# Rows broadcast through DRAM instead of on GpSimd, with merge and router issued in written order

## The chip, the cores and the metric

The kernel runs on one core of a Trainium2 chip. The metric is the device time of one execution in microseconds (us), as the median of the timed runs. Engines are named as in the profile: PE (TensorE), DVE (VectorE), ACT (ScalarE), POOL (GpSimd) and SP (SyncE, whose queue issues every DMA of this kernel).

## What is computed

One encoder layer for 256 tokens of width 1024, in float32:

```
mod = silu(c) @ w_ada + b_ada          # six rows of 1024: shift, scale, gate, twice
h   = x * (1 + scale1) + shift1
z   = h @ w_in                         # q, k, v of branch A; low-rank q, kv of branch B; gates g_a, g_b
y_a, y_b = chunked attention, latent attention
merged = sigmoid(g_a) * (y_a @ w_branch_a) + sigmoid(g_b) * (y_b @ w_branch_b)
x = layer_norm(2**0.25 * x + gate1 * (merged @ w_out), ln1_g, ln1_b)
h = x * (1 + scale2) + shift2
f = mixture of experts: top 4 of 32 by h @ w_router + b_router, clamped SwiGLU experts
x = layer_norm(2**0.25 * x + gate2 * f, ln2_g, ln2_b)
```

The expert weights are by far the most data: 32 experts of three 1024x1024 matrices, 402.7 MB. All of them are read.

## The kernel before

SBUF holds twenty blocks of 128x2048 float32 (1024 KB each). Every weight goes through them: `al()` gives the block that was freed longest ago, `fr()` frees one, and `hold(4)` sets four aside for the first expert loads. A load can start only when the last reader of its block is done. SP issues the DMAs in one queue, so a load that waits for its block keeps the later ones back.

The work comes in stages. The attention stage computes z and both attentions; a weight is split there into a rounded part and a rest (`split`, L152 to L154: ACT casts, then DVE or POOL subtracts, as its argument says), and `mm3` (L278 to L281) makes three matmuls of it. `ada2` gathers the modulation rows on DVE, and `z_pair` makes the gate columns g0 to g7.

The **merge** follows, and it is where the change lies. `mod_rows` (L714) sums the modulation rows on PE, adds the bias on DVE, and writes the second shift and scale to a DRAM buffer `rowd`, from which four small loads bring them back as columns. `load_branch(jp)` loads and splits a quarter of both branch weights. The loop over jp (L773) makes tiles ba and bb on PE (48 matmuls of 256 columns, four banks of PSUM for two quarters), multiplies them by the gates on DVE (L788 to L790) and splits the result into mgh and mgl. `mod_gates` (L733) spreads the rows gate1 and gate2 over 128 partitions with four `partition_broadcast` on POOL, called at jp 1. `mod_cols` (L745) scales the router's weights, and `mod_sums` (L756) makes two row sums on PE.

Then **output projection and router**: `load_wo` loads and splits a quarter of w_out, `o_part(t, hf, i)` is 12 matmuls of 512 columns for token half t and column half hf, `resid` adds the residual, `r_T` transposes it and makes router logits, `stats`, `normalise` and `route` make the normalised x (`xn`), the choice of experts and the one-hot matrix `pt0`, `gather_first` gathers the tokens of the first two experts (tiles sxg), `weigh` and `first_norm` make the routing weights and the residual of the second norm.

The **experts** run in 14 groups: s, then e0 to e12. A group loads gate, up and down weights in 1024 KB blocks (L1012) and computes tiles sg, su, sd (L1056). Here the gathered tokens are first scaled into `xgb` (L1044 on ACT, L1046 on DVE). `load_norm` at the end spreads ln2_g and ln2_b with two more `partition_broadcast`.

What sets the order: the kernel is built with a scheduler that simulates time and moves instructions within each engine, SP's DMAs among them, as

```
with _tile.TileContext(nc, schedule_with_timeline_sim=True) as tc:
```

says, and `tc.issue_after` bounds it at two places.

Of the kernel before, what the change touches and what calls it, by code (L numbers as in the profile page):

```python
# [70 lines left out]
def tile_layer(  # L71
# [583 lines left out]

    def load_branch(jp):
# [21 lines left out]
    for i in range(4):  # L678
# [6 lines left out]
        if i == 3:  # L685
            ms_v, ms_r = al()
# [28 lines left out]
    def mod_rows():  # L715
# [46 lines left out]

    G.memset(ones_p, 1.0)
    mod_rows()
    hold(4)
    load_branch(1)
    for b in range(2):
        A.activation(gT[b], gT[b], AF.Sigmoid)
    mgh_v, mgh_r = al(F32R)
    mgl_v, mgl_r = al(F32R)  # L770
    mgh = mgh_v.rearrange("p (j n) -> p j n", j=8)
    mgl = mgl_v.rearrange("p (j n) -> p j n", j=8)
    for jp in range(4):  # L773
# [9 lines left out]
        if jp + 2 < 4:  # L783
            load_branch(jp + 2)
# [7 lines left out]
        if jp == 1:  # L792
            rwa_v, rwa_r = al()
            gate1, g1r = rwa_v[:, 0:D], rwa_v[:, D:2 * D]
            b1r = p3.tile([P, D], F32, name="b1r")
            SP.dma_start(g1r, bcast_rows(ln1_g[0]))
            SP.dma_start(b1r, bcast_rows(ln1_b[0]))
            mod_gates()
        if jp == 2:
            mod_cols()  # L800
        if jp == 3:
            mod_sums()
            for j in range(3):
                G.tensor_copy(sel0[32 * j:32 * j + 32, :, :], ident[0:E, E - 2:E].unsqueeze(2).to_broadcast([E, 2, CAP]))
# [3 lines left out]
    WO = []  # L808

    def load_wo(hf, i):  # L810
        v, r = al()
        v = v.rearrange("p (k m) -> p k m", k=4)
        SP.dma_start(v, w_out[0, i * 512:(i + 1) * 512, hf * 512:(hf + 1) * 512].rearrange("(k p) m -> p k m", p=P))
        hv, hr = al(F32R)
        lv, lr = al(F32R)
        hi = hv.rearrange("p (k m) -> p k m", k=4)
        lo = lv.rearrange("p (k m) -> p k m", k=4)
        for q in range(2):
            ks = slice(2 * q, 2 * q + 2)
# [39 lines left out]
    def r_T(t, hf):  # L859
        ps = ps_b(f"rT{t}_{hf}")  # L860
        for q in range(2):
# [3 lines left out]
            A.copy(rT[:, 4 * hf + 2 * q:4 * hf + 2 * q + 2, :].rearrange("p a n -> p (a n)"), ps[:, q * 256:(q + 1) * 256])  # L865
        if hf == 0:
            lgps.append(ps_b(f"lg{t}"))
        for k in range(4 * hf, 4 * hf + 4):
            last = T.matmul(lgps[t][:, 0:E], rT[:, k, :], wrs[:, k, 0, :], start=(k == 0), stop=(k == 7))
        return last  # L870

    def stats(t):
# [15 lines left out]
    def route(t):  # L888
# [11 lines left out]
        ps = ps_b(f"cum{t}")  # L900
        if t == 1:
            T.matmul(ps[:, 0:E], ones_bf, mask_bf[:, 0, :], start=True, stop=False)
        T.matmul(ps[:, 0:E], tri, mask_bf[:, t, :], start=(t == 0), stop=True)
        V.tensor_mul(posm[:, t, :], ps[:, 0:E], mask_bf[:, t, :])
        last = V.tensor_tensor(pt0[:, t, :].rearrange("p (a n) -> p a n", a=2),
                        iota_s[:, 0:CAP].unsqueeze(1).to_broadcast([P, 2, CAP]),
                        posm[:, t, E - 2:E].unsqueeze(2).to_broadcast([P, 2, CAP]), op=ALU.is_equal)
        m8s.append(m8)
        ohs.append(oh)
        return last  # L910
# [23 lines left out]

    def gather_first(t):
# [9 lines left out]
    G.memset(zero_bf, 0.0)  # L945
    for i in range(2):
# [3 lines left out]
        load_wo(1, i)  # L950
# [4 lines left out]
    r_T(0, 0)  # L955
    resid(0, 1)
    o_part(1, 1, 0)
    fr(*WO[2][2:4])
    stats(0)
    r_T(0, 1)  # L960
    r_T(1, 0)
    o_part(1, 1, 1)
    fr(*WO[3][2:4])
    normalise(0)
    route(0)
    resid(1, 1)
    r_T(1, 1)
    gather_first(0)
    stats(1)
    routed = route(1)  # L970
    normalise(1)
# [17 lines left out]
    xgb = [mp.tile([P, 8, P], F32, name=f"xgb{i}") for i in range(2)]  # L989
# [35 lines left out]
    def expert_group(nm, segs, slots, wcol, get_w, get_bias, hooks=(), end=None):  # L1025
# [6 lines left out]
        for i in range(2):  # L1032
            if slots is not None:
# [5 lines left out]
            else:  # L1039
                ps = gps[i]  # L1040
            for kk in range(4):
                k = 4 * i + kk
                if kk % 2 == 0:
                    A.activation(xg[:, k, :], ps[:, kk * P:(kk + 1) * P], AF.Identity, bias=bc[:, k:k + 1], scale=gc[:, k:k + 1])  # L1044
                else:
                    V.tensor_scalar(xg[:, k, :], ps[:, kk * P:(kk + 1) * P], gc[:, k:k + 1], bc[:, k:k + 1],  # L1046
                                    op0=ALU.mult, op1=ALU.add)
# [192 lines left out]
    def load_norm():  # L1240
        fin_v, o_v = al()[0], al()[0]
        lnr = o_v[0:1, :].rearrange("p (a n) -> p a n", a=2)
        SP.dma_start(lnr[:, 0, :], ln2_g)
        SP.dma_start(lnr[:, 1, :], ln2_b)
# [130 lines left out]
```

## Time and profile before

| | |
|---|---|
| median of 3 runs | 1246.0 us (1244.69 to 1246.91) |
| profiled execution: its time | 1242.76 us |
| profiled execution: its span, first to last instruction | 1241.1 us |
| PE busy, share of the span | 1096.4 us, 88% |
| DVE, ACT, POOL busy | 375.4, 180.5, 102.2 us |
| mean granted TensorE clock | 0.954 of full speed |
| DMA moved | 462.51 MB |

The span begins with the first instruction; all positions below are microseconds from there. The attention stage ends at about 198 us, merge, projection and router run to about 284 us, and the experts from there to the end. A row of the trace gives start, duration, engine, line, operation and tiles, how many instructions it merges, and in brackets how long the engine sat idle before and what ended that.

### The profile page before, as it was taken

To read this page: it belongs to the slowest core of one execution; us is meant where nothing else is said; L and a number is where in the kernel's file an instruction comes from. 1 tells how busy PE (TensorE), PEld (TensorE's weight loads), DVE (VectorE), ACT (ScalarE), POOL (GpSimd) and SP (SyncE) were. 2 spreads that over 40 slices of the span, in tenths; PEclk is the share of its full clock that TensorE was granted. 3 is DMA by queue.
4 is the path that set the end of the run, shared out by engine and by line. 5 is a ranking of instruction groups with operands and counts; after the bars stand their busy time and mean duration, and the time that the engine had idled before them with its cause. 6 is when DMAs were issued, how large, how long until landed. Compare 5 with 4: busy or idle time off the path is not lost.

```text
span 1241.1 us, 19489 instructions
## 1 busy us (share of the span) xinstructions
PE 1096.4 (88%) x7991; PEld 534.1 (43%) x7991; DVE 375.4 (30%) x752; ACT 180.5 (15%) x364; POOL 102.2 (8%) x126
## 2 busy tenths in 40 slices
PE   5889896788898999999989889888898989898995
PEld 4659886763243333534323232232233434343431
DVE  4768984564122121212111011020021212121213
ACT  3346454321000000000000000000000000000011
POOL 2211553310000000000000000000000000000000
PEclk8989998889999999799999999999999999998998
DMA  9969567398999999999999999999999999999991
GB/s 339 321 214 331 179 232 244 136 400 322 418 419 419 418 419 419 419 419 419 418 420 419 421 417 420 419 420 419 418 420 418 419 419 418 420 419 418 420 389 67
DMA packets 93281, 462.51 MB, mean 373 GB/s; under 512 B 11499, under 2 KB 36120, under 8 KB 42246
## 3 DMA queue, kind: packets, MB, share of 16 engines
q1 hardware_dynamic: 93190, 461.24, 92.4%
q8 instruction: 64, 1.05, 0.3%
q14 instruction: 27, 0.22, 0.0%
HBM read 460.15 MB, written 1.06 MB: 372 GB/s over the span
## 4 chain that ended last, share of the span: by engine, by line
DMA 43%; PE 42%; DVE 7%; issue 2%; SPq 2%; ACT 2%; POOL 1%; ACTq 0%; DVEq 0%; POOLq 0%
DMA blk<-in_w_up_dram 14%; DMA blk<-in_w_gate_dram 13%; DMA blk<-in_w_down_dram 13%; DVE blk L642 1%; PE e11d L1056 1%; PE e12u L1056 1%; PE e1d L1056 1%; PE sd L1056 1%; PE e12d L1056 1%; PE e3d L1056 1%; PE e3g L1056 1%; PE e2d L1056 1%; PE e0d L1056 1%; PE e12g L1056 1%; PE e0u L1056 1%
## 5 line engine op out<-in xcount | busy, mean ns | idle before, releaser
L154 POOL TENSOR_TENSOR blk<-blk,blk 128x512 fp32r<-128x512 f32 (+2 forms) x44 | 82.6, 1895 | 145.1 <-ACT blk L153 71.7
L1303 POOL COPY sel<-sel 96x64 bf16<-96x64 bf16 (+2 forms) x30 | 5.9, 229 | 837.4 <-PE e6d L1136 90.5
L153 ACT CAST blk<-blk 128x512 fp32r<-128x512 f32 (+2 forms) x76 | 54.0, 766 | 62.1 <-DVE blk L790 16.2
L154 DVE TENSOR_TENSOR blk<-blk,blk 128x512 fp32r<-128x512 f32 (+2 forms) x32 | 43.7, 1377 | 30.3 <-ACT blk L153 21.1
L1096 ACT ACTIVATE blk<-blk 128x512 f32<-128x512 f32 x28 | 17.2, 630 | 218.0 <-DVE blk L1094 217.9
L642 DVE SCALAR_TENSOR_TENSOR blk<-blk,csil,blk 128x1024 f32<-128x1024 f32 x28 | 41.3, 1509 | 0.0
L279 PE MATMUL g<-blk,blk 128*128 128x256 f32 x128 | 38.7, 302 | 2.3 <-ACT blk L153 2.3
L281 PE MATMUL g<-blk,blk 128*128 128x256 f32 x128 | 38.6, 304 | 1.8 <-POOL blk L154 1.4
L280 PE MATMUL g<-blk,blk 128*128 128x256 f32 x128 | 38.3, 300 | 0.0
L1056 PE MATMUL e6u<-blk,blk 128*32 128x512 f32 x128 | 25.4, 599 | 4.1 <-DMA blk<-in_w_up_dram 4.1
L1056 PE MATMUL e7u<-blk,xgb 128*32 128x512 f32 x128 | 25.4, 599 | 4.1 <-DMA blk<-in_w_up_dram 4.1
L1056 PE MATMUL e5u<-blk,xgb 128*32 128x512 f32 x128 | 25.3, 599 | 4.1 <-DMA blk<-in_w_up_dram 4.1
L281 PEld LDWEIGHTS g<-blk,blk 128*128 128x128 f32 x128 | 26.2, 206 | 3.6 <-POOL blk L154 1.6
L279 PEld LDWEIGHTS g<-blk,blk 128*128 128x128 f32 x128 | 26.5, 207 | 2.8 <-ACT blk L153 2.5
L280 PEld LDWEIGHTS g<-blk,blk 128*128 128x128 f32 x128 | 26.5, 207 | 0.8 <-issue 0.8
L1056 PE MATMUL e4d<-blk,blk 128*32 128x512 f32 x128 | 23.0, 642 | 2.9 <-DMA blk<-in_w_down_dram 2.9
L1056 PE MATMUL e5d<-blk,xgb 128*32 128x512 f32 x128 | 22.8, 598 | 3.1 <-DMA blk<-in_w_down_dram 2.8
L1056 PE MATMUL e7d<-blk,blk 128*32 128x512 f32 x128 | 22.7, 598 | 3.1 <-DMA blk<-in_w_down_dram 2.8
L1056 PE MATMUL e6d<-blk,xgb 128*32 128x512 f32 x128 | 22.8, 636 | 2.7 <-DMA blk<-in_w_down_dram 2.7
L281 PE MATMUL bb<-blk,blk 128*128 128x256 f32 x32 | 10.7, 334 | 14.1 <-POOL blk L154 14.1
L1056 PE MATMUL e6g<-blk,blk 128*32 128x512 f32 x128 | 20.8, 596 | 1.7 <-DMA blk<-in_w_gate_dram 1.7
L1056 PE MATMUL e7g<-blk,xgb 128*32 128x512 f32 x128 | 19.8, 596 | 1.7 <-DMA blk<-in_w_gate_dram 1.7
(741 smaller groups left out, 1937.3 us busy)
## 6 DMA issues: line engine op xcount, KB each, us to landing
blk<-in_w_gate_dram SPq DMA_DIRECT2D x128, 1024.0 KB
blk<-in_w_up_dram SPq DMA_DIRECT2D x128, 1024.0 KB
blk<-in_w_down_dram SPq DMA_DIRECT2D x126, 1024.0 KB
blk<-in_w_ada_dram SPq DMA_DIRECT2D x24, 1024.0 KB
blk<-in_w_in_dram SPq DMA_DIRECT2D x12, 1024.0 KB
blk<-in_w_in_dram SPq DMA_DIRECT2D x8, 592.0 KB
blk<-in_w_out_dram SPq DMA_DIRECT2D x4, 1024.0 KB
blk<-in_w_branch_a_dram SPq DMA_DIRECT2D x4, 512.0 KB
```

The source lines that it names most:

```text
L153: A.copy(hi, src)
L154: (V if eng == "V" else G).tensor_sub(lo, src, hi.bitcast(F32))
L279: T.matmul(o, sh, mh, start=first, stop=False)
L280: T.matmul(o, sh, ml, start=False, stop=False)
L281: T.matmul(o, sl, mh, start=False, stop=last)
L642: eng.scalar_tensor_tensor(acc_v[:, sl], v[:, q * D:(q + 1) * D], csil[:, k:k + 1], acc_v[:, sl], op0=ALU.mult, op1=ALU.add)
L1056: T.matmul(pss[hf][c0:c0 + m, :], stat[:, k, c0:c0 + m], ch[par][k // 2][:, k % 2, hf * 512:(hf + 1) * 512], start=(k == 0), stop=(fine an ...
L1096: A.activation(s, g[:, sl], AF.Sigmoid, scale=SW_ALPHA)
L1303: G.tensor_copy(sel[:, lo:lo + n], sel96[:, r:r + 1].to_broadcast([96, n]))
```

## The change

POOL's broadcasts go. `rowd` gets four rows; gate1 and gate2 are loaded from it, and ln2_g and ln2_b from their inputs, by DMAs that read one row for all 128 partitions (`bcast_rows`). From `mod_rows` to `first_norm` the order of PE, ACT, DVE and POOL is the order in which the code is written (`tc.manual_schedule`); SP's order is still the scheduler's. Loading and splitting of branch and output weights are separate functions, and the raw loads are called earlier. `mod_cols` moves behind the merge loop. Logits, counting and placing are functions of their own, and the first tokens' scaling (`evacuate`) is called ahead of `weigh` and `first_norm`, in the written part.

```diff
     def load_branch(jp):
...
+        WB_raw.append((v, r))
+
+    def split_branch(jp):
+        v, r = WB_raw[jp]
         hv, hr = al(F32R)
...
         if i == 3:
-            load_branch(0)
+            split_branch(0)
+            load_branch(1)
...
-        rowd = dram.tile([2, D], F32, name="rowd")
-        for i in range(2):
+        rowd = dram.tile([4, D], F32, name="rowd")
+        for n, (st, j) in enumerate(((0, 2), (1, 0), (0, 0), (1, 2))):
             for hf in range(2):
-                j = 2 * (1 - i) + hf
-                SP.dma_start(rowd[i:i + 1, hf * 512:(hf + 1) * 512], rows32[32 * j:32 * j + 1, i, :])
+                SP.dma_start(rowd[n:n + 1, hf * 512:(hf + 1) * 512], rows32[32 * (j + hf):32 * (j + hf) + 1, st, :])
...
-    def mod_gates():
-        for i, dst in enumerate((gate1, gate2)):
-            for hf in range(2):
-                j = 2 * i + hf
-                G.partition_broadcast(dst[:, hf * 512:(hf + 1) * 512], rows32[32 * j:32 * j + 1, i, :])
+        SP.dma_start(gate1, bcast_rows(rowd[2]))
+        SP.dma_start(gate2, bcast_rows(rowd[3]))
...
+    engines = {e.engine for e in (T, A, V, G)}
+    order_cm = tc.manual_schedule(engines=engines)
+    order_cm.__enter__()
     G.memset(ones_p, 1.0)
...
     mod_rows()
-    hold(4)
-    load_branch(1)
+    split_branch(1)
     for b in range(2):
         A.activation(gT[b], gT[b], AF.Sigmoid)
+    load_branch(2)
+    split_branch(2)
+    hold(4)
...
-        if jp + 2 < 4:
-            load_branch(jp + 2)
+        if jp == 0:
+            load_branch(3)
+            split_branch(3)
+        else:
+            load_wo((jp - 1) // 2, (jp - 1) % 2)
...
-            mod_gates()
-        if jp == 2:
-            mod_cols()
-        if jp == 3:
-            mod_sums()
...
+        if jp in (1, 2):
+            split_wo()
+    mod_cols()
+    mod_sums()
...
     gather_first(1)
+    xg0 = keep.tile([P, 8, P], F32, name="xgb0")
+    evacuate(xg0, gps)
     for t in range(2):
-        with tc.issue_after(routed.ins):
-            weigh(t)
+        weigh(t)
     for t in range(2):
-        with tc.issue_after(routed.ins):
-            first_norm(t)
+        first_norm(t)
+    order_cm.__exit__(None, None, None)
...
-        G.partition_broadcast(g2r, lnr[:, 0, :])
-        G.partition_broadcast(b2r, lnr[:, 1, :])
+        SP.dma_start(g2r, bcast_rows(ln2_g[0]))
+        SP.dma_start(b2r, bcast_rows(ln2_b[0]))
```

Three places show what the new order is. The first is DVE at the start of the merge, before (tiles mod are the modulation rows, ba and bb the first quarter's products, L154 a split's subtraction):

```order
L721 TENSOR_TENSOR blk_180_1825<-mod_0_1987,blk_180_1825 128x512
L154 TENSOR_TENSOR blk_216_2075<-blk_214_2071,blk_215_2074 128x1024
L721 TENSOR_TENSOR blk_180_1825<-mod_1_1993,blk_180_1825 128x512
L788 TENSOR_TENSOR blk_133_1257<-blk_133_1257,ba_2021 128x512
L154 TENSOR_TENSOR blk_208_2012<-blk_206_2008,blk_207_2011 128x1024
L789 TENSOR_TENSOR blk_165_1608<-blk_165_1608,bb_2022 128x512
L790 TENSOR_TENSOR blk_133_1257<-blk_133_1257,blk_165_1608 128x512
L747 TENSOR_SCALAR c_98<-c_98 128x16
```

and DVE at the same place in the changed kernel (blk_194, blk_211 and blk_219 are the raw weights of quarters 1, 2 and 3):

```order
L729 TENSOR_TENSOR blk_181_1828<-mod_0_1994,blk_181_1828 128x512
L729 TENSOR_TENSOR blk_181_1828<-mod_1_2000,blk_181_1828 128x512
L154 TENSOR_TENSOR blk_209_2022<-blk_194_1908,blk_208_2021 128x1024
L154 TENSOR_TENSOR blk_213_2033<-blk_211_2029,blk_212_2032 128x1024
L154 TENSOR_TENSOR blk_221_2096<-blk_219_2092,blk_220_2095 128x1024
L824 TENSOR_TENSOR blk_133_1257<-blk_133_1257,ba_2042 128x512
L825 TENSOR_TENSOR blk_165_1608<-blk_165_1608,bb_2043 128x512
L826 TENSOR_TENSOR blk_133_1257<-blk_133_1257,blk_165_1608 128x512
```

The splits of quarters 1, 2 and 3 now all stand ahead of the first multiplication by a gate, and the column work (L747) is gone from here.

The second is SP's queue in the same stretch, before (c is the tile of columns, blk_220 quarter 3's raw weights, blk_224 the rows gate1 and ln1_g):

```order
L727 DMA rowd<-blk_180_1825 1x512 x2
L660 DMA blk_220_2135<-in_w_branch_a_dram 128x4x256
L727 DMA rowd<-blk_180_1825 1x512 x2
L660 DMA blk_220_2135<-in_w_branch_b_dram 128x4x256
L730 DMA c_98<-rowd 128x8
L731 DMA c_98<-rowd 128x8x1
L730 DMA c_98<-rowd 128x8
L731 DMA c_98<-rowd 128x8x1
L796 DMA blk_224_2149<-in_ln_g_dram 128x1024
L813 DMA blk_234_2282<-in_w_out_dram 128x4x512
```

and SP's queue in the changed kernel (blk_219 is quarter 3, blk_225 and blk_231 the first two quarters of w_out):

```order
L734 DMA rowd<-blk_181_1828 1x512 x8
L737 DMA c_98<-rowd 128x8
L738 DMA c_98<-rowd 128x8x1
L737 DMA c_98<-rowd 128x8
L738 DMA c_98<-rowd 128x8x1
L739 DMA blk_205_1992<-rowd 128x1024
L740 DMA gate_1983<-rowd 128x1024
L662 DMA blk_219_2092<-in_w_branch_a_dram 128x4x256
L662 DMA blk_219_2092<-in_w_branch_b_dram 128x4x256
L791 DMA blk_225_2156<-in_w_out_dram 128x4x512
L791 DMA blk_231_2219<-in_w_out_dram 128x4x512
```

Quarter 3 stood between the row writes and ahead of the column loads; it now stands behind eight row writes, four column loads and the two broadcasts.

The third is DVE at the end of the router, before (w, nm are `weigh`'s tiles, x_sb is written by `first_norm`; the scaling L1046 of the first tokens comes 23 instructions further on):

```order
L905 TENSOR_TENSOR pt_2302<-iota_s,posm 128x128
L916 TENSOR_SCALAR w_0_2574<-m_0_2495 128x4
L916 TENSOR_SCALAR w_1_2586<-m_1_2550 128x4
L929 SCALAR_TENSOR_TENSOR x_sb<-xn,blk_224_2149 128x1024 x2
L919 RECIPROCAL w_0_2574<-w_0_2574 128x4
L919 RECIPROCAL w_1_2586<-w_1_2586 128x4
L931 SCALAR_TENSOR_TENSOR x_sb<-b1r,x_sb 128x1024 x2
```

and in the changed kernel:

```order
L928 TENSOR_TENSOR pt_2305<-iota_s,posm 128x128
L962 TENSOR_SCALAR xgb_2578<-sxg_2527,c_98 128x128 x2
L962 TENSOR_SCALAR xgb_2578<-sxg_2529,c_98 128x128 x2
L936 TENSOR_SCALAR w_0_2587<-m_0_2494 128x4
L939 RECIPROCAL w_0_2587<-w_0_2587 128x4
L940 TENSOR_TENSOR w_0_2587<-w_0_2587 128x4
```

The scaling of the first tokens follows directly on the one-hot matrix pt, and `weigh` and `first_norm` come behind it.

## Rows read from the trace of the kernel before

**Rows 1.** Page: GB/s moved, in 40 slices of 31.0 us.
```profile
GB/s 339 321 214 331 179 232 244 136 400 322 418 419 419 418 419 419 419 419 419 418 420 419 421 417 420 419 420 419 418 420 418 419 419 418 420 419 418 420 389 67
```
**Rows 2.** Windows: stretch, its us, engines' busy us, clock, DMA share, GB/s.
```profile
240.00:280.00 40.00, 34.12 (x177) 28.95 (x175) 26.57 (x76) 10.04 (x18) 7.36 (x3) 0.88 0.95 368
280.00:300.00 20.00, 17.05 (x138) 7.12 (x141) 10.70 (x30) 2.10 (x7) 0.00 (x0) 0.90 0.70 275
```
**Rows 3.** Timeline of SP's queue: issues of loads, merge to first experts.
```profile
199.71 0.55 SPq L727 DMA_DIRECT2D rowd<-blk  x2
...
204.27 0.46 SPq L730 DMA_DIRECT2D c<-rowd  x1
...
206.85 1.18 SPq L796 DMA_DIRECT2D blk<-in_ln_g_dram  x1
223.83 17.03 SPq L813 DMA_DIRECT2D blk<-in_w_out_dram  x3
...
246.71 0.37 SPq L813 DMA_DIRECT2D blk<-in_w_out_dram  x1
...
256.41 18.96 SPq L1012 DMA_DIRECT2D blk<-in_w_up_dram  x8
277.02 22.34 SPq L1012 DMA_DIRECT2D blk<-in_w_down_dram  x8
```
**Rows 4.** Timeline of POOL in the merge.
```profile
199.09 2.41 POOL L154 TENSOR_TENSOR blk<-blk,blk 128x1024 fp32r<-128x1024 f32 x1 [4.25 <-PE mod L719]
208.11 1.48 POOL L737 PARTITION_BROADCAST gate<-blk  x2 [6.61 <-DMA c<-rowd]
217.26 2.33 POOL L154 TENSOR_TENSOR blk<-blk,blk 128x1024 fp32r<-128x1024 f32 x1 [7.67 <-issue]
225.32 1.48 POOL L737 PARTITION_BROADCAST blk<-blk  x2 [5.73 <-issue]
233.62 5.83 POOL L154 TENSOR_TENSOR blk<-blk,blk 128x1024 fp32r<-128x1024 f32 x2 [6.82 <-issue]
```
**Rows 5.** Timeline of PE: three stops, and two projection matmuls.
```profile
219.64 0.58 PE L281 MATMUL bb<-blk,blk 128*128 128x256 f32 x1 [9.48 <-POOL blk L154]
...
236.01 0.38 PE L281 MATMUL bb<-blk,blk 128*128 128x256 f32 x1 [4.58 <-POOL blk L154]
...
241.18 0.39 PE L279 MATMUL o<-blk,blk 128*128 128x512 f32 x1
...
241.64 0.39 PE L281 MATMUL o<-blk,blk 128*128 128x512 f32 x1
...
288.58 1.92 PE L1056 MATMUL sg<-blk,xgb 128*32 128x512 f32 x16 [2.95 <-DVE xgb L1046]
```
**Rows 6.** Chain of waits, around the last gate columns and into the merge.
```profile
180.06 5.95 DMA blk<-in_w_branch_a_dram
...
192.13 0.21 PE g L279
...
196.13 0.12 PE g L279
...
197.93 1.04 PE mod L719 x8
```
**Rows 7.** Timeline of DVE: splits, column work, end of the router.
```profile
199.60 2.98 DVE L154 TENSOR_TENSOR blk<-blk,blk 128x1024 fp32r<-128x1024 f32 x1
...
209.14 0.47 DVE L747 TENSOR_SCALAR c<-c 128x16 f32<-128x16 f32 x1 [1.97 <-DMA c<-rowd]
...
221.84 1.04 DVE L754 TENSOR_REDUCE wrsum<-wrs 128x64 f32<-128x512 f32 x1
...
246.94 1.23 DVE L154 TENSOR_TENSOR blk<-blk,blk 128x1024 fp32r<-128x1024 f32 x1 [0.26 <-ACT blk L153]
...
279.75 3.76 DVE L929 SCALAR_TENSOR_TENSOR x_sb<-xn,blk 128x1024 f32<-128x1024 f32 x2
```
**Rows 8.** Groups by line and form, 195 to 290 us: count, busy, mean ns, idle before.
```profile
L788 DVE TENSOR_TENSOR blk<-blk,ba 128x512 f32<-128x512 f32 x4 | 2.7, 677 | 0.1
```

More of the change, by code (lines that the diff above doesn't have):

```diff
@@ L654, in tile_layer @@
     WB = []
+    WB_raw = []
     def load_branch(jp):
@@ L685, in tile_layer @@
         if i == 3:
+            load_branch(0)
             ms_v, ms_r = al()
@@ L772, in tile_layer, with load_wo, split_wo @@
     mgl = mgl_v.rearrange("p (j n) -> p j n", j=8)
+    WO, WO_raw = [], []
+    def load_wo(hf, i):
+        v, r = al()
+        v = v.rearrange("p (k m) -> p k m", k=4)
+        SP.dma_start(v, w_out[0, i * 512:(i + 1) * 512, hf * 512:(hf + 1) * 512].rearrange("(k p) m -> p k m", p=P))
+        WO_raw.append((v, r))
+    def split_wo():
+        v, r = WO_raw[len(WO)]
+        hv, hr = al(F32R)
+        lv, lr = al(F32R)
+        hi = hv.rearrange("p (k m) -> p k m", k=4)
+        lo = lv.rearrange("p (k m) -> p k m", k=4)
+        for q in range(2):
+            ks = slice(2 * q, 2 * q + 2)
+            split(v[:, ks, :], hi[:, ks, :], lo[:, ks, :], "VG"[q])
+        fr(r)
+        WO.append((hi, lo, hr, lr))
     for jp in range(4):
@@ L865, in r_T, with logits @@
             A.copy(rT[:, 4 * hf + 2 * q:4 * hf + 2 * q + 2, :].rearrange("p a n -> p (a n)"), ps[:, q * 256:(q + 1) * 256])
+    def logits(t, hf):
         if hf == 0:
@@ L868, in r_T @@
         for k in range(4 * hf, 4 * hf + 4):
-            last = T.matmul(lgps[t][:, 0:E], rT[:, k, :], wrs[:, k, 0, :], start=(k == 0), stop=(k == 7))
-        return last
+            T.matmul(lgps[t][:, 0:E], rT[:, k, :], wrs[:, k, 0, :], start=(k == 0), stop=(k == 7))
     def stats(t):
@@ L933, in tile_layer, with evacuate @@
     gps = []
+    def evacuate(xg, banks):
+        for k in range(8):
+            src = banks[k // 4][:, (k % 4) * P:(k % 4 + 1) * P]
+            if k % 2 == 0:
+                A.activation(xg[:, k, :], src, AF.Identity, bias=bc[:, k:k + 1], scale=gc[:, k:k + 1])
+            else:
+                V.tensor_scalar(xg[:, k, :], src, gc[:, k:k + 1], bc[:, k:k + 1], op0=ALU.mult, op1=ALU.add)
     def gather_first(t):
@@ L945, in tile_layer @@
     G.memset(zero_bf, 0.0)
+    for j in range(3):
+        G.tensor_copy(sel0[32 * j:32 * j + 32, :, :], ident[0:E, E - 2:E].unsqueeze(2).to_broadcast([E, 2, CAP]))
     for i in range(2):
@@ L949, in tile_layer @@
         fr(*WO[i][2:4])
-        load_wo(1, i)
+        load_wo(1, i) if i else None
+        split_wo()
     for t in range(2):
@@ L955, in tile_layer @@
     r_T(0, 0)
+    logits(0, 0)
     resid(0, 1)
@@ L958, in tile_layer @@
     fr(*WO[2][2:4])
+    r_T(0, 1)
+    logits(0, 1)
+    r_T(1, 0)
     stats(0)
-    r_T(0, 1)
-    r_T(1, 0)
+    for hf in range(2):
+        normalise(0, hf)
     o_part(1, 1, 1)
     fr(*WO[3][2:4])
-    normalise(0)
     route(0)
+    count(0)
     resid(1, 1)
     r_T(1, 1)
+    for hf in range(2):
+        logits(1, hf)
+    place(0)
     gather_first(0)
     stats(1)
-    routed = route(1)
-    normalise(1)
+    normalise(1, 1)
+    route(1)
+    normalise(1, 0)
+    count(1)
+    place(1)
     gather_first(1)
+    xg0 = keep.tile([P, 8, P], F32, name="xgb0")
+    evacuate(xg0, gps)
     for t in range(2):
-        with tc.issue_after(routed.ins):
-            weigh(t)
+        weigh(t)
     for t in range(2):
-        with tc.issue_after(routed.ins):
-            first_norm(t)
+        first_norm(t)
+    order_cm.__exit__(None, None, None)
     fr(mgh_r, mgl_r, rt_r, ms_r, rwa_r)
@@ L988, in tile_layer @@
     late = {}
-    xgb = [mp.tile([P, 8, P], F32, name=f"xgb{i}") for i in range(2)]
+    xgb = [xg0, mp.tile([P, 8, P], F32, name="xgb1")]
     turn = [0]
@@ L1031, in expert_group @@
             slots(pt)
-        for i in range(2):
-            if slots is not None:
+            banks = []
+            for i in range(2):
                 ps = ps_b(f"{nm}xg{i}")
@@ L1038, in expert_group @@
                         T.matmul(ps[:, kk * P:(kk + 1) * P], xn[:, t, k, :], pt[:, t, :], start=(t == 0), stop=(t == 1))
[L1039 to L1047, printed above, removed]
+                banks.append(ps)
+            evacuate(xg, banks)
         def mm(stat, kind, name):
```

66 lines of the change are left out of this document (25 added, 41 removed).

## The prediction

> **What bounds the kernel now.** I read the 40 slices of the page first. From slice 10 on the DMA engines move about 419 GB/s until the last weights are in [rows 1]: the experts' stream is as fast as this kernel ever gets it, and the end of the run follows the stream. Faster computing among the experts buys nothing; what counts is how much of the stream has landed when it becomes continuous. Before that, slice 8 (217 to 248 us) moves only 136 GB/s and slice 10 still misses a quarter. So the reader should look at the windows next: 368 GB/s in 240 to 280, 275 in 280 to 300 [rows 2].
>
> I count in blocks of 1024 KB (1.049 MB), 2.50 us each at 419 GB/s. From 240 to 300 the windows give 14.7 + 5.5 = 20.2 MB, 19.3 blocks. Two of them are w_out: the third of the three issues that begin at 223.83 ends at 240.86, and one more goes at 246.71 [rows 3]. With the four held gate blocks, 17.3 + 4 = **21.3 expert blocks have landed at 300 us**. That number is what the change has to beat.
>
> Two things keep it low. SP shows that the up loads begin only at 256.41, and that eight down loads need 22.34 us to issue where eight up loads need 18.96 [rows 3]: they wait for blocks that sg frees, and sg stands still until 288.58, for DVE's scaling of the first tokens [rows 5]. DVE has `weigh` and `first_norm` in front of it, beginning with 3.76 us of L929 [rows 7]. The other is in the merge: PE stops for 9.48 and 4.58 us for a subtraction on POOL [rows 5]. POOL's own timeline tells why. Its two pairs of broadcasts take 1.48 us each, but there are 6.61, 7.67, 5.73 and 6.82 us of idleness around them, mostly ended by nothing that the profile shows, as if each change to the broadcast and back cost about 6 to 7 us [rows 4]. Split weights queue behind it.
>
> **The change, part by part.** *Broadcasts.* All of the 26.8 us of idle time on POOL can go; on PE it is at most 9.48 + 4.58 = 14.1 us. What is late next is the written order on DVE, worked out now.
>
> *Up to the merge.* ACT no longer waits for the first branch weights in front of the last gate columns; that wait is 5.95 us of the chain [rows 6]. But ACT now copies g6 before it casts g7's weights, and POOL's subtraction still stands behind, so I take only 1.2 us: mod begins at 196.7 instead of 197.93 [rows 6], lasts 1.9 as two tiles of 1.04 less overlap, and the merge's first matmul comes at 198.6. Bounds: 0 to 4.
>
> *First half of the merge.* The quarters 0 and 1 are 96 matmuls at 0.12 us, the pitch of the gate columns at full clock [rows 6]: 11.5 us, to 210.1. Then PE needs a bank back, so DVE must have multiplied quarter 0. DVE now does that behind the split of quarter 3, whose load stands in SP's queue behind the rows. DVE's two additions of 0.7 make the rows ready at about 199.4; eight writes at half of 0.55 us end at 201.6; the four columns take 206.85 - 204.27 = 2.6 us [rows 3], to 204.2; two broadcasts at the 1.18 us of the like load of ln1_g at most [rows 3], to 206.3; quarter 3 is issued by 207. Ahead of it in the engines are 1 MB of broadcasts, itself 1 MB: 5 us, so the half that DVE needs lands near 209.5 and a cast and a subtraction (1.05, an estimate from the pitch of ACT's work beside DVE's 1.23 [rows 7]) bring DVE to the first multiplication at 211.8. Bounds: 208, if the broadcasts cost nothing beside the stream, and 217, if quarter 3 needs the 5.95 us that the first quarter's load needed [rows 6], and DVE's split 2.98 instead of 1.23 [rows 7]. PE resumes at 212.4: a stop of 2.3 us where 9.48 stood.
>
> *Second half.* A quarter costs DVE three operations of 0.68 [rows 8], ACT's cast and a subtraction, 3.4 us in line. PE is the later one: 96 matmuls from 212.4 take 11.5 us, and 2 more because PE came back from a stop at a pitch of 0.21, half of its clock, before [rows 6]: 226.0. Quarter 3's own 3.4 follow, 229.5. Then come the column operations, which were hidden at 209 to 211 [rows 7] and now stand on the path: 0.47 for the first, 1.04 for the reduction [rows 7], about 1.2 for the five between, and 0.5 for PE's sums: 3.2. **w_out's first matmul comes at 232.7**; before, the fourth or so starts at 241.18 [rows 5].
>
> *Projection.* The blocks of the up loads are mostly those that w_out's split halves held. I call X the moment at which the first half of o_part(1, 1) is done, since the stream becomes continuous then. To X there are 72 + 12 matmuls at 0.23 us (two from 241.18 to 241.64 [rows 5]), 19.3 us, and eight transposes and eight logits with two waits for ACT's copies, about 3, and 1 for a cold start: **X = 256**. That is no earlier than the up loads of before, 256.41 [rows 3]. But one block more has been issued by then: gates 4 held + 4, and one up, all landed before 247, where before the fourth gate is still under way. So 9 blocks at X. With 1.5 us to first data, at 300 us 9 + (300 - 257.5) / 2.50 = **26.0 blocks**, if nothing stops.
>
> *End of the router.* From the end of o_part(1, 1), X + 4.3, I add residual, transpose, copies, logits and gather of half 0 (9), one count, place and gather of half 1 (4), and a scaling: sg begins at X + 18 = 274, 14.6 us earlier than 288.58. The stream then asks for sg's first freed blocks at about X + 20 and gets them at X + 21.5; another block is that of gate1 and ln1_g, read by `first_norm`, which now ends some 10 us after the scaling, and the queue reaches it at about that time. I charge 2.5 us for both, between 0 and 6.
>
> *At the end of the run* ln2's rows now move 1 MB behind the last weights, 2.5 us, beside the last group's matmuls. Cost nothing; 1 us if they delay them.
>
> Sum: (26.0 - 21.3) x 2.50 = 11.8, less 2.5, is **9.3 us**. The profiled execution would go from 1242.76 to 1233.5; the median of the runs shown stands 3.2 above it, so 1246.0 becomes **1236.7**. The likeliest case alone, by X between 253 and 260, is 1233 to 1241.
>
> **A rule that speaks against it.** DVE's split takes 1.23 us alone at 246.94, and 2.98 at 199.60 [rows 7], where POOL's own ran from 199.09 to 201.50 [rows 4]. So the two hold each other up, and the written order puts DVE's and POOL's halves of each split next to each other. This is a rival of its own below. [...]
>
> **The rivals.**
>
> *DVE and POOL collide on the path (0.16).* Three splits lie on DVE's path before X (quarter 3, w_out 0 and 1). Each that starts beside POOL's costs 2.98 - 1.23 = 1.75 more: 5.3 us on X. For it: the two rows. Against it: ACT casts DVE's half first, so DVE is a cast ahead of POOL. Time: 1236.7 + 5.3 = 1242.
>
> *No late stops (0.17).* The broadcasts land beside the stream, quarter 3 arrives at 208, PE keeps its clock: X is 252, and `first_norm` frees its block in time. Gain 11.8 + 4 + 0, near 16: 1230. For it: the DMA engines have room there, slice 8 moves a third of what they can [rows 1]. Against it: the columns and PE's sums are on the path whatever happens.
>
> [...]
>
> *SP's queue holds the merge (0.08), slower.* Quarter 3 and w_out stand behind the row writes, columns and broadcasts, and each of these needs what DVE has just summed. If 128 reads of one row go far below stream speed, quarter 3 is late, DVE's first multiplication is late, and everything behind it. Price: one for one. When DVE's half lands at 218.8 instead of 209.5, the gain is gone; from 221.3 the kernel is slower, and at 224.5 it stands at 1252. For it: the column loads, 4 KB each, are all issued before 206.85 and reach their reader at 209.14 [rows 3, 7], so this path is slow for its size. Against it: those go in pieces of a few bytes, the broadcasts in rows of 4 KB.
>
> That the change does not do what it says is no case: no broadcast is left in POOL's order.
>
> **How the numbers follow.** Forecast 0.49, rivals 0.16, 0.17, 0.10, 0.08. A measurement of this kernel can tell 0.2%, 2.5 us, from no change. Faster: 0.49 + 0.16 + 0.17 = 0.82; same 0.10; slower 0.08. The range takes in most of the two faster rivals and of the unknown costs (0 to 4 at the merge's start, -4 to +5 at quarter 3, 0 to 6 of late stops): 1229 to 1244.
>
> **What would show it.** In the changed trace POOL has no idle stretch of 6 us between splits. PE stops once after quarter 1, by 2 to 3 us, for DVE, and once before w_out, by 5 to 7 us. The up loads begin near 256, sg near 274 without a stop, and slices 9 and 10 carry more. DMA engines idle from about 247 to 256. I am wrong if X is later than 264, or if the stream shows a gap of over 6 us after it.

## The result, and the profile after

The changed kernel takes **1239.0 us** (median of five, 1238.98 to 1240.54) against 1246.0 (1244.36 to 1247.25) for the kernel before on the same chip: ratio 0.9948, 95% interval 0.9934 to 0.9963. The forecast was 1236.7. The profiled executions lie closer together: 1239.56 us now, 1242.76 before, a gain of 3.2 us where the working had 9.3. Further runs of the kernel before, beside the experiments, had medians of 1245.35, 1243.68 and 1244.13.

So the time came out near the forecast, but the trace does not follow its steps. PE still stops twice in the merge, and the stops are long (timeline of PE after: start, duration, engine, line, operation; in brackets the idle time before and what ended it):

```profile
195.78 1.93 PE L727 MATMUL mod<-blk,ones 128*32 128x512 f32 x16
218.30 0.55 PE L279 MATMUL ba<-blk,blk 128*128 128x256 f32 x1 [8.90 <-DVE blk L824]
218.66 0.42 PE L280 MATMUL ba<-blk,blk 128*128 128x256 f32 x1
218.87 0.41 PE L281 MATMUL ba<-blk,blk 128*128 128x256 f32 x1
...
239.14 0.69 PE L761 MATMUL gb<-wrsum,ones_p 128*128 128x64 f32 x2 [6.84 <-DVE wrsum L757]
239.59 0.77 PE L279 MATMUL o<-blk,blk 128*128 128x512 f32 x1
...
279.10 13.94 PE L1092 MATMUL sg<-blk,xgb 128*32 128x512 f32 x128
```

Stops of 9.48 and 4.58 for POOL [rows 5] have become 8.90 and 6.84 for DVE. The first w_out matmul comes at 239.59, 0.8 us earlier than before (240.39), where 8 were forecast. But sg starts at 279.10 and runs through, where it stood still until 288.58 [rows 5].

The queue shows what DVE waited for (timeline of SP after):

```profile
197.63 7.63 SPq L734 DMA_DIRECT2D rowd<-blk  x8
205.37 0.35 SPq L737 DMA_DIRECT2D c<-rowd  x1
...
208.01 0.38 SPq L740 DMA_DIRECT2D gate<-rowd  x1
208.48 0.38 SPq L662 DMA_DIRECT2D blk<-in_w_branch_a_dram  x1
...
263.02 8.21 SPq L1055 DMA_DIRECT2D blk<-in_w_up_dram  x6
```

Eight row writes of 2 KB hold the queue for 7.63 us. The columns, broadcasts and quarter 3 follow in line. The chain of waits after continues from there, through ACT's cast into DVE's line:

```profile
208.48 6.67 DMA blk<-in_w_branch_a_dram
215.26 1.05 ACT blk L153
216.33 1.23 DVE blk L154
217.56 0.60 DVE blk L824
...
226.92 0.60 DVE blk L824
...
232.59 0.60 DVE blk L824
```

Quarter 3's first half lands 6.67 us after its issue, and the first multiplication (L824), behind its split, starts at 217.5. From there the chain stays on DVE and ACT, with 4.57, 4.79 and 5.67 us from one quarter to the next (the last is 226.92 to 232.59). The windows answer to [rows 2]:

```profile
240.00:280.00 40.00, 35.87 (x196) 28.88 (x198) 22.79 (x69) 7.72 (x14) 3.71 (x2) 0.95 0.66 256
280.00:300.00 20.00, 20.00 (x182) 5.91 (x176) 14.75 (x35) 2.51 (x8) 0.00 (x0) 1.00 1.01 417
```

From 240 to 280 the DMA engines move less than before, 256 against 368 GB/s; from 280 on the stream is whole, 417 against 275. Ahead of that more has moved, 218 GB/s in 200 to 240 against 114. The net shows at the loads of the next group, whose first issue moves from 303.04 to 298.51 (SP, before and then after):

```profile
303.04 6.64 SPq L1012 DMA_DIRECT2D blk<-in_w_gate_dram  x4
```
```profile
298.51 10.81 SPq L1055 DMA_DIRECT2D blk<-in_w_gate_dram  x8
```

That is 4.5 us of stream; the span fell by 3.3. In the prediction's count 4.5 us are 1.8 blocks, so about 23.1 blocks had landed at 300 us (an estimate from these two rows), against 21.3 before and 26.0 forecast.

### The profile page after: what moved, and what is told of

It is laid out like the page before. It is cut to its first block, busy times and chain, and to the rows that moved or that the text cites. A ratio compares the mean times of both kernels' runs of the same rounds, so it can differ in the third digit from the quotient of the medians.

```text
span 1237.8 us, 19474 instructions
## 1 busy us (share of the span) xinstructions
PE 1095.9 (89%) x7991; PEld 522.6 (42%) x7991; DVE 375.2 (30%) x751; ACT 179.6 (15%) x363; POOL 96.2 (8%) x120
## 4 chain that ended last, share of the span: by engine, by line
DMA 47%; PE 33%; DVE 5%; issue 1%; ACT 1%; SPq 0%; POOL 0%; ACTq 0%; DVEq 0%; another core or an unknown queue 0%
DMA blk<-in_w_down_dram 19%; DMA blk<-in_w_gate_dram 14%; DMA blk<-in_w_up_dram 13%; PE su L1092 1%; PE e2d L1092 1%; PE e1d L1092 1%; PE sd L1092 1%; PE e12d L1092 1%; PE e3g L1092 1%; PE e3d L1092 1%; PE e2g L1092 1%; PE e0d L1092 1%; PE sg L1092 1%; PE e4g L1092 1%; PE e0u L1092 1%; PE e1u L1092 1%
## 5 line engine op out<-in xcount | busy, mean ns | idle before, releaser
L154 POOL TENSOR_TENSOR blk<-blk,blk 128x512 fp32r<-128x512 f32 (+2 forms) x44 | 81.9, 1880 | 154.8 <-ACT blk L153 98.6
L154 DVE TENSOR_TENSOR blk<-blk,blk 128x512 fp32r<-128x512 f32 (+2 forms) x32 | 38.1, 1200 | 29.0 <-ACT blk L153 26.1
L281 PE MATMUL g<-blk,blk 128*128 128x256 f32 x128 | 37.4, 295 | 1.6 <-POOL blk L154 0.9
L279 PE MATMUL g<-blk,blk 128*128 128x256 f32 x128 | 37.6, 294 | 1.2 <-ACT blk L153 1.2
L280 PE MATMUL g<-blk,blk 128*128 128x256 f32 x128 | 37.2, 291 | 0.0
L281 PEld LDWEIGHTS g<-blk,blk 128*128 128x128 f32 x128 | 25.0, 197 | 3.3 <-POOL blk L154 1.3
L279 PEld LDWEIGHTS g<-blk,blk 128*128 128x128 f32 x128 | 25.1, 196 | 1.9 <-ACT blk L153 1.4
L280 PEld LDWEIGHTS g<-blk,blk 128*128 128x128 f32 x128 | 25.1, 196 | 1.2 <-issue 1.2
L1092 PE MATMUL e4d<-blk,blk 128*32 128x512 f32 x128 | 23.3, 656 | 2.5 <-DMA blk<-in_w_down_dram 2.2
L1092 PE MATMUL e5g<-blk,xgb 128*32 128x512 f32 x128 | 19.8, 595 | 1.7 <-DMA blk<-in_w_gate_dram 1.7
```

Of the source, the lines that this page charges most:

```text
L154: (V if eng == "V" else G).tensor_sub(lo, src, hi.bitcast(F32))
L279: T.matmul(o, sh, mh, start=first, stop=False)
L280: T.matmul(o, sh, ml, start=False, stop=False)
L281: T.matmul(o, sl, mh, start=False, stop=last)
L1092: T.matmul(pss[hf][c0:c0 + m, :], stat[:, k, c0:c0 + m], ch[par][k // 2][:, k % 2, hf * 512:(hf + 1) * 512], start=(k == 0), stop=(fine an ...
```

## The experiments

Each kernel was timed 4 to 12 times, beside runs of the kernel before; "ratio" is its time over theirs, with the 95% interval. "Merge" is the time from the first ba matmul to the first o matmul; where it starts moves by up to 6 us between kernels whose attention stage is the same, so the length is compared.

| kernel | us | ratio to before | merge | stops of PE in it |
|---|---|---|---|---|
| before | 1246.0 | 1 | 40.7 | 9.48, 4.58 |
| after | 1239.0 | 0.9948 (0.9934 to 0.9963) | 42.0 | 8.90, 6.84 |
| split3_late | 1236.1 | 0.9939 (0.9919 to 0.9960) | 38.9 | 3.40, 10.02 |
| cols_early | 1233.8 | 0.9908 (0.9892 to 0.9925) | 34.8 | 9.05 |
| pool_rows | 1235.2 | 0.9919 (0.9904 to 0.9935) | 34.0 | 0.30, 9.71 |
| split3_cols | 1230.0 | 0.9890 (0.9876 to 0.9904) | 31.3 | 3.22, 2.42, 0.25 |
| q3_early | 1234.9 | 0.9923 (0.9909 to 0.9936) | 34.5 | 10.73 |
| q3_early_cols | 1224.0 | 0.9846 (0.9832 to 0.9859) | 25.2 | 1.17, 0.25 |
| merge_sched | 1226.6 | 0.9865 (0.9849 to 0.9880) | 23.3 | none |
| before_dma_rows | 1224.4 | 0.9829 (0.9813 to 0.9844) | 23.3 | none |
| before_gates_only | 1224.3 | 0.9845 (0.9826 to 0.9863) | 23.3 | none |
| rows_scale_first | 1224.3 | 0.9839 (0.9825 to 0.9852) | 23.3 | none |
| evac_last | 1243.9 | 1.0001 (0.9983 to 1.0019) | 43.4 | 10.40, 7.52 |

Differences below are of medians. By the ratios those against the changed kernel are 1.1 us for split3_late, 3.1 for q3_early, 3.6 for pool_rows, 5.0 for cols_early, 7.2 for split3_cols, 12.7 for q3_early_cols, 14.8 for before_dma_rows, and 6.6 the other way for evac_last.

**The broadcasts alone** (before_dma_rows): the kernel before, with only this changed (and four rows in `rowd` instead of two):

```diff
...
-                G.partition_broadcast(dst[:, hf * 512:(hf + 1) * 512], rows32[32 * j:32 * j + 1, i, :])
+        SP.dma_start(gate1, bcast_rows(rowds[0][2]))
+        SP.dma_start(gate2, bcast_rows(rowds[0][3]))
...
-        G.partition_broadcast(g2r, lnr[:, 0, :])
-        G.partition_broadcast(b2r, lnr[:, 1, :])
+        SP.dma_start(g2r, bcast_rows(ln2_g[0]))
+        SP.dma_start(b2r, bcast_rows(ln2_b[0]))
```

> The kernel before with the broadcasts alone replaced: all six rows go through DRAM as in the changed kernel, the scheduler keeps the order of every engine. Theory A (POOL's idle time around the broadcasts is what PE waits for): PE's stops of 9.48 and 4.58 us shrink to under 3 each, the first o comes 5 to 10 us earlier, but sg still waits for DVE's weighing, so the time is 1238 to 1243. Theory B (the rows' way through SP's queue takes the place of the broadcasts, as it does in the changed kernel, where the eight row writes lasted 7.63 us): the quarter-3 load is issued after 206, a stop of 6 us or more stands in the merge, time 1244 to 1248. Theory C (the written order is all of the gain): 1244 to 1247 with the stops gone.

All three theories missed: **20.9 us** less than the kernel before, timed beside it. PE runs from 201.44 to the first o at 224.71 without a stop, and the sums gb follow the last product at once. SP of this kernel shows the same late row path, and why it hurts no one here:

```profile
201.43 4.89 SPq L726 DMA_DIRECT2D rowd<-blk  x8
...
208.39 0.58 SPq L660 DMA_DIRECT2D blk<-in_w_branch_a_dram  x1
...
240.75 15.29 SPq L1013 DMA_DIRECT2D blk<-in_w_up_dram  x8
```

Quarter 3 is issued at 208.39, as late as in the changed kernel, but ahead of the broadcasts, and DVE has quarter 0 multiplied by 209.5, before it arrives (ACT's first cast of it starts at 212.65). The up loads begin at 240.75, 15.7 us earlier than before [rows 3]. So the rest of the change, the written order with the calls that it moves, costs 1239.0 - 1224.4 = 14.6 us.

**Which broadcasts** (before_gates_only: ln2's two rows left on POOL).

> The kernel before with gate1 and gate2 through DRAM as in the changed kernel, ln2's two rows left to POOL's broadcasts at the end. Theory A (all of the 20.9 us that the rows through DRAM gave the kernel before come from the merge): 1223 to 1226. Theory B (POOL's broadcasts at the end hold up the last groups or the last norm): 1227 to 1232. Theory C (the rows of ln2 through DMA cost 1 MB of stream, 2.5 us, at the end): 1220 to 1222.

1224.3: theory A. The rows at the end show no worth either way, as the prediction had it: the medians differ by 0.2 us, the ratios by 2.0, and their intervals overlap.

**Broadcasts back, written order kept** (pool_rows; `rowd` then has four row writes instead of eight):

```diff
...
-        SP.dma_start(gate1, bcast_rows(rowd[2]))
-        SP.dma_start(gate2, bcast_rows(rowd[3]))
...
         if jp in (1, 2):
             split_wo()
+        if jp == 1:
+            mod_gates()
```

> The changed kernel with gate1 and gate2 again spread by four broadcasts on POOL, in written order at jp 1 behind the split of the first w_out quarter; four row writes are left, and SP issues quarter 3's load ahead of the column loads. Theory A (every change between POOL's broadcast and its other work costs 6 to 7 us): about 20 us stand on POOL between the first w_out split and the second, whose POOL half ends near 250 instead of 234; PE stops for it in the projection, and the time is 1242 to 1250. Theory B (a broadcast costs only its own 1.5 us, the idle time around it was waiting): POOL loses 6 us or less, quarter 3 lands 2 to 4 us earlier because of the shorter queue, PE's stop after quarter 1 is 5 to 7 us instead of 8.90, time 1235 to 1238.

POOL's timeline shows the price that theory A sets, though the time is that of B:

```profile
219.96 2.44 POOL L154 TENSOR_TENSOR blk<-blk,blk 128x1024 fp32r<-128x1024 f32 x1 [6.59 <-ACT blk L153]
228.04 1.87 POOL L744 PARTITION_BROADCAST blk<-blk  x2 [5.64 <-DVE blk L830]
229.77 1.47 POOL L744 PARTITION_BROADCAST gate<-blk  x2
238.35 2.38 POOL L154 TENSOR_TENSOR blk<-blk,blk 128x1024 fp32r<-128x1024 f32 x1 [7.10 <-issue]
```

Between two splits stand 16 us (theory A had 20), of which the broadcasts are 3.3. They have no idle time between them, 5.64 before and 7.10 behind. Neither gap is a wait that the kernel asks for: the multiplication named for the 5.64 stands later in the code than the broadcast, and the cast that the next split needs was done at 225.50. So the price is paid at the change to the broadcast and at the change back, 5.64 and 7.10 us here, as the 6.61, 7.67, 5.73 and 6.82 of the kernel before had suggested [rows 4]. What POOL does in that time the trace does not show. The price cost no time here, because PE waited 9.71 us for DVE ahead of w_out anyway, and the late split came without a stop in the projection. With four row writes instead of eight (1.37 us) quarter 3 was issued at 201.41, and the first stop was 0.30 where theory B had 5 to 7. With its POOL broadcasts this kernel is 3.8 us faster than the changed one, 3.6 by the ratios (the intervals just touch).

**Quarter 3's place on DVE** (split3_late):

```diff
             load_branch(3)
-            split_branch(3)
...
+        if jp == 0:
+            split_branch(3)
```

> The changed kernel with one call moved: quarter 3 is still loaded after quarter 0, but its split stands behind quarter 0's multiplications and split. Theory A (PE's stop of 8.90 us is on the path of the end, one for one, because DVE has quarter 3's late half in front of L824): the stop after quarter 1 falls below 1.5 us, a stop of 2 to 3 us for quarter 3's weights comes before ba3, bb3 ends at 224 to 227 instead of 232.30, the first o at 231 to 234, the up loads begin at 255 to 258 instead of 263.02, and the time is 1231 to 1235. Theory B (the wait only moves: PE stops before ba3 for the same late load): bb3 ends at 230 or later and the time is 1237 to 1240. Theory C (the start of the up loads is not what the time follows): they begin before 258 and the time stays within 1 us of 1239.

The stop of 8.90 went, one of 3.40 came before ba3, bb3 ended at 224.72; so far theory A. Then the wait for wrsum grew to 10.02, and of the 4 to 8 us of theory A 2.9 are left by the medians, 1.1 by the ratios, whose intervals overlap: no gain is shown.

**The column operations** (cols_early):

```diff
-    mod_cols()
+        if jp == 1:
+            mod_cols()
     mod_sums()
```

> The changed kernel with the column operations (mod_cols) called at jp 1 instead of behind the merge loop; PE's two sums stay where they are. Theory A (the column operations are 3 us of the path): wrsum is ready before bb3 ends, PE's stop before w_out falls from 6.84 to about 4 us, first o at 236 to 237 instead of 239.59, up loads near 260, time 1235 to 1237. Theory B (the 2.4 us that DVE now spends earlier delay quarter 3's or w_out's splits by as much): first o stays within 1 us of 239.6, time 1238 to 1240.

5.3 us, more than theory A. PE's stop of 6.84 is gone entirely (gb stands without a bracket):

```profile
222.13 0.55 PE L279 MATMUL ba<-blk,blk 128*128 128x256 f32 x1 [9.05 <-DVE blk L824]
...
235.80 0.33 PE L761 MATMUL gb<-wrsum,ones_p 128*128 128x64 f32 x2
```

The split of quarter 3's own product, which the prediction had put in the path before w_out, is not needed by the first half of o.

**Both** (split3_cols).

> The changed kernel, all of it in written order, with both single moves: quarter 3's split behind quarter 0's multiplications and the column operations at jp 1. Theory A (the two costs add): 1239.0 less 2.9 and 5.3 is 1230 to 1232. Theory B (they overlap, since the later quarters' multiplications and splits on DVE, 5.7 us a quarter in line, are late next and hold the second half of o): 1233 to 1237, with a stop inside o.

1230.0, theory A (7.2 us by the ratios, where the single moves have 1.1 and 5.0): the time that the first move frees now counts, since the wait for wrsum no longer takes it back (2.42 instead of 10.02).

**Quarter 3's place on SP** (q3_early; and q3_early_cols, with the column operations at jp 1 as well):

```diff
     load_branch(2)
     split_branch(2)
+    load_branch(3)
     hold(4)
...
         if jp == 0:
-            load_branch(3)
             split_branch(3)
```

> The changed kernel with the load of quarter 3 called one step earlier, behind that of quarter 2, so that SP issues it ahead of the row writes (it then also issues the first w_out load before the column loads). All engines keep their written order; quarter 3's split still stands in front of quarter 0's multiplications on DVE. Theory A (the 8.90 us stop is quarter 3 arriving late behind the rows on SP): the stop after quarter 1 falls to 0 to 2 us and PE keeps its clock, the way from the merge's first matmul to the first o falls from 42.0 to 31 to 34 us, what is left of the stop before w_out is 6 to 9 us for wrsum, and the time is 1229 to 1233. Theory B (the place of the split in DVE's order is the cost, wherever the load stands): the stop stays over 6 us and the time within 2 us of 1239.

> The same early load of quarter 3 and the column operations at jp 1, all else of the changed kernel in written order. Theory A (these two places are the whole cost of the written order in the merge): 23 to 26 us from the merge's first matmul to the first o, as the scheduler's order has, and 1223 to 1227. Theory B (DVE's line of 5.7 us a quarter is late next): stops of 2 us or more for quarter 2's or 3's product inside o, 27 us or more, 1227 to 1231.

With the load ahead of the rows the stop of 8.90 is gone, though the split still stands in front of the multiplications. So the place of the split costs nothing by itself. The stop needs both, a late load and its split in front: split3_late, which moves the split alone, ends it too, but PE then waits 3.40 for the same load. The early load alone is worth 4.1 us (3.1 by the ratios), and its 1234.9 lies between the two theories: the wait for wrsum takes over at 10.73, where theory A had 6 to 9. The chain of q3_early shows the same pattern once more, with a quarter of w_out as the late load:

```profile
213.16 8.85 DMA blk<-in_w_out_dram
...
222.09 1.05 ACT blk L153
...
223.17 1.23 DVE blk L154
224.40 0.60 DVE blk L824
```

Its split stands ahead of quarter 3's multiplications on DVE, and the column operations behind them. With both (timeline of PE, q3_early_cols):

```profile
222.21 0.43 PE L761 MATMUL gb<-wrsum,ones_p 128*128 128x64 f32 x2 [1.17 <-DVE wrsum L757]
222.90 0.47 PE L279 MATMUL o<-blk,blk 128*128 128x512 f32 x1 [0.25 <-DVE blk L824]
```

The merge takes 25.2 us and the kernel 1224.0; the interval of its ratio overlaps that of before_dma_rows: these two places are **nearly all of the 15 us** that the written order cost (by the ratios 12.7 of 14.8).

**Written order only behind the merge** (merge_sched: `order_cm.__enter__()` stands behind the loop).

> The changed kernel with the written order beginning behind the merge loop instead of ahead of it: merge and column operations are ordered by the scheduler, projection and router as written. It also puts quarter 3's load ahead of the row writes on SP. Theory A (the written order costs in the merge and pays in the router): from the merge's first matmul to the first o it takes 23 to 26 us, as in the kernel before with its rows through DRAM alone (23.3), not 42.0; sg runs without the stop of 3.51 us that it has there, so the stream has no gap after 250, and the time is 1218 to 1222. Theory B (the router's written order is worth nothing): 1223 to 1226. Theory C (what the scheduler does well in the merge rests on loads called late, and the raw loads called earlier spoil it): 27 us or more to the first o, 1228 to 1239.

The merge is as short as with the scheduler's order (o then stops for 1.93, 0.84 and 0.36 us), and sg runs without a stop, but the time is 1226.6, none of the three. Up loads were issued from 236.11 on, yet only 291 GB/s moved in 240 to 250 and 302 in 250 to 260 (418 and 420 in before_dma_rows). SP's waits from 236 to 262 name the block (line, waited for, us in total, times, longest):

```profile
SPq L1055 <- PE o L281: 10.5, 1, 10.5
```

The second up load got a block that the projection's matmuls were still reading, and was issued at 246.79; in before_dma_rows the second goes at 244.51, and no wait for o there is longer than 3.6. What the order of the blocks alone would bring, no run tests.

**First tokens' scaling.** evac_last puts `evacuate(xg0, gps)` behind `first_norm` in the changed kernel; rows_scale_first puts it ahead of `weigh` in before_dma_rows.

> The changed kernel with the first tokens' scaling put back behind the weighing and the first norm in the written order. Theory A (scaling first is what keeps sg from stopping, and its blocks feed the stream): sg waits 7 to 10 us longer for xgb, the stream shows a gap of 4 to 7 us between 275 and 295, time 1243 to 1246. Theory B (the blocks freed by sg are not the ones the stream waits for at that moment): the gap stays under 2 us and the time within 1238 to 1241.

> The kernel before with all rows through DRAM (1224.4 us) and one part of the change beside it: the first tokens' scaling stands ahead of the weighing and the first norm on DVE; the scheduler keeps all other order. Theory A (the late stop of sg costs the stream what evac_last cost the changed kernel, 4.9 us at most): sg runs without the stop of 3.51 us, the window that carried 257 GB/s in 270 to 280 carries over 380, and the time is 1219 to 1222, the best of all. Theory B (the stream waits there for another block, such as that of the first norm, which now ends later): the gap stays or moves, 1223 to 1227.

In the changed kernel the place is worth 4.9 us (6.6 by the ratios), theory A: sg starts 7.6 us later and stops when the scaling comes last (PE and window of evac_last):

```profile
286.73 1.92 PE L1092 MATMUL sg<-blk,xgb 128*32 128x512 f32 x16 [1.25 <-ACT xgb L960]
294.68 5.61 PE L1092 MATMUL sg<-blk,xgb 128*32 128x512 f32 x28 [6.02 <-DVE cnt L1191]
```
```profile
280.00:300.00 20.00, 12.19 (x78) 6.14 (x81) 12.82 (x34) 2.43 (x8) 0.00 (x0) 0.77 0.66 255
```

255 GB/s stand where 417 stood. (This profiled execution took 1251.0 us against a median of 1243.9, so the gap of the median may be smaller.) In the faster kernel the same move shows no gain, theory B: the stop of sg goes, but in 260 to 280 the stream only rises from 338 to 363 GB/s (windows of before_dma_rows, then rows_scale_first). 25 GB/s over 20 us is 0.5 MB, 1.2 us:

```profile
260.00:280.00 20.00, 15.07 (x122) 6.67 (x125) 12.49 (x38) 2.36 (x8) 0.00 (x0) 0.91 0.84 338
```
```profile
260.00:280.00 20.00, 17.66 (x151) 8.01 (x153) 13.71 (x41) 2.40 (x8) 0.00 (x0) 0.91 0.90 363
```

## Why the prediction was right, and where not

*The frame held.* The end follows the experts' stream: from after to q3_early_cols the first o moves by 239.59 - 222.90 = 16.7 us and the time by 15.0. It is the stream that counts, and not the first o by itself: merge_sched has it 19.8 us earlier than after and gains 12.4.

*The start of the merge* was right: first ba matmul at 197.64 (198.6 forecast), quarters 0 and 1 done at 209.41 (210.1).

*Quarter 3 is the step that failed.* "Eight writes at half of 0.55 us" took 7.63 instead of 2.2. The price of a write was right (0.23 us each, see the end); what the sum has at nothing is a wait between them. The row of [rows 3] from which 0.55 came has two writes issued back to back; in the changed kernel the eight waited for earlier loads, 5.5 us in all (waits of SP after: line, waited for, us in total, times, longest):

```profile
SPq L734 <- DMA blk<-in_w_gate_dram: 2.3, 1, 2.3
SPq L734 <- DMA blk<-in_w_branch_a_dram: 1.8, 1, 1.8
SPq L734 <- DMA blk<-in_w_branch_b_dram: 1.4, 1, 1.4
```

The columns took 1.9 instead of 2.6. (The working's next step has a slip: two broadcasts at 1.18 from 204.2 end at 206.6, not 206.3. Nothing hangs on it, as it goes on from 207.) Quarter 3 was issued at 208.48 where 207 stood, and its first half, given 2.5 us, needed 6.67 behind the broadcasts. L824 came at 217.5 against 211.8, just past the upper bound of 217, and the stop was 8.90, not 2.3. PE came back at half pitch as forecast: 0.21 from 218.66 to 218.87, with a granted clock of 0.66 over 210 to 220, and the 24 ba matmuls take 5.4 us against 3.1 in quarter 0.

*DVE's line in the second half* is another term that was too small. The prediction's 3.4 us for a quarter's own product leave out w_out's split, which follows in the same line behind quarters 1 and 2, and POOL's hold on L826 (below); from quarter 2 to quarter 3 the chain shows 5.67. It cost little here, as PE, late itself, ends bb3 at 232.30 and DVE starts on quarter 3 at 232.51. In pool_rows, where PE is early, the line is much the same (5.66 at that place), and PE waits 9.71 for its end.

*The second stop* was forecast at 5 to 7 and measured at 6.84. What I did not see is that it need not be there: the column operations, called at jp 1, fit into DVE's idle time (cols_early).

*X* was 263.2 instead of 256, the sum of these errors. No row shows two small terms of the working, 1 us for a cold start and 1.5 us to first data. In the changed kernel ten matmuls of o stood about 0.43 us apart before the pitch was 0.23 (239.59 to 243.96), some 2.1 us more; and from the up load's issue at 263.02 nothing moved until 263.5, then 16 GB/s until 264.0 and 229 in the half us behind it. *The end of the router* was better than forecast: sg at X + 15.9, not X + 18, and no late stop, where 2.5 us were charged. That gave part of the 7 us back; 4.9 us is what evac_last measures for the scaling's place in the changed kernel.

*From the profile to the median.* 3.2 us were added because the profiled execution of before lay below its median. That of after lies 0.5 above its median. The 1236.7 came near 1239.0 partly by this luck: by the profiles the forecast was 1233.5 and the result 1239.56, a third of the forecast gain.

*The rivals.* "SP's queue holds the merge", given 0.08, is the mechanism that acted: by its one-for-one price a landing at 215.2 (208.48 + 6.67) instead of 209.5 takes 5.7 us of the 9.3; without the 2.5 for late stops that leaves 6.1, which is 1239.9. It stopped short of its turning point, 218.8. The same time, given 0.10, did not come: X was late, at 263.2, but sg ran through. "Collide", given 0.16, acted too, but elsewhere: the splits on DVE's path take their lone 1.23, while three of the four L826 are longer by 1.23, 0.89 and 0.84 us, 3.0 in sum where 5.3 were priced (last section).

*What the prediction did not ask* is what each part would bring alone. It put PE's loss to POOL at 14.1 us and then built everything on the written order. The broadcasts alone shorten the merge by 17.4 us: the two stops, and 3.3 more, which goes with the matmuls at half pitch behind them (0.21 instead of 0.12 us from 220.02 to 222.58, and again from 236.35 on).

## What to carry to other kernels

When a change removes a cost and also fixes an order by hand, price the removal under the old order first: here it was worth 21 us and the new order gave 15 of them back. In a written order, ask of every load what stands ahead of it in its queue and waits for a result just made, and put work that needs only early data (here the column operations) ahead of work that needs late data. A wait removed in line shows the next one: of the single moves here the best gave 5 us and one no gain that is shown, the right pair 15.

## What the runs showed of the hardware

DVE and POOL did hold each other up, but not with every operand. In the changed kernel POOL's split runs from 217.79 to 220.15. DVE's multiplications L824 and L825, with one operand in PSUM, keep their 0.68 beside it; L826, with both in SBUF, takes 1.92 (timelines of POOL and DVE after):

```profile
217.79 2.36 POOL L154 TENSOR_TENSOR blk<-blk,blk 128x1024 fp32r<-128x1024 f32 x1 [11.71 <-ACT blk L153]
226.74 2.44 POOL L154 TENSOR_TENSOR blk<-blk,blk 128x1024 fp32r<-128x1024 f32 x1 [6.59 <-ACT blk L153]
232.41 2.38 POOL L154 TENSOR_TENSOR blk<-blk,blk 128x1024 fp32r<-128x1024 f32 x1 [3.23 <-ACT blk L153]
```

```profile
217.48 0.68 DVE L824 TENSOR_TENSOR blk<-blk,ba 128x512 f32<-128x512 f32 x1
218.07 0.68 DVE L825 TENSOR_TENSOR blk<-blk,bb 128x512 f32<-128x512 f32 x1
218.79 1.92 DVE L826 TENSOR_TENSOR blk<-blk,blk 128x512 f32<-128x512 f32 x1
...
223.36 0.69 DVE L826 TENSOR_TENSOR blk<-blk,blk 128x512 f32<-128x512 f32 x1
...
228.15 1.58 DVE L826 TENSOR_TENSOR blk<-blk,blk 128x512 f32<-128x512 f32 x1
...
233.82 1.53 DVE L826 TENSOR_TENSOR blk<-blk,blk 128x512 f32<-128x512 f32 x1
```

At 223.36, without POOL's split beside it, the same takes 0.69; at 228.15 and 233.82, beside the next two splits, 1.58 and 1.53. All three end 0.55 or 0.56 us after POOL's split does, as if most of their 0.69 had waited for its end: 220.71 against 220.15, 229.73 against 229.18, 235.35 against 234.79. POOL was held as well: in before_dma_rows its split takes 2.40 us at 215.22, and 2.88 at 227.54, beside two of DVE's splits (226.95 to 230.96).

A small write costs little; what stands ahead of it in the queue can cost more. One write of 2 KB takes SP 0.21 to 0.29 us in the kernels before and after (rows of both: count, shortest, median and longest in ns, first and last start):

```profile
L727 SPq DMA_DIRECT2D rowd<-blk x4: 219/241/262, 199.7 to 203.5; - x4
```
```profile
L734 SPq DMA_DIRECT2D rowd<-blk x8: 214/232/293, 197.6 to 205.1; - x8
```

Eight are then some 1.9 us. The rest of the 7.63 lies between them, most of it in three waits for the three loads issued just ahead (2.3, 1.8 and 1.4 us). In the three kernels with two more loads of 512 KB ahead the eight take 9.30 (q3_early), 9.17 (q3_early_cols) and 9.48 (merge_sched); merge_sched has five such waits, 7.5 us. In before_dma_rows they take 4.89, and SP waits there for DVE's additions (3.4 us), for no load. Four writes behind three loads take 1.37 and wait for no load either (pool_rows). Why a write waits for a load of which it needs nothing, no run tests.
